# A decode step of a hybrid decoder in other parts: which engine forms the key-value product, who adds the old state, and when the decay is applied

## The chip, the cores and the metric

The kernel runs on one core of a Trainium2 chip. A core has five engines that run side by side and wait for each other by semaphores: TensorE (PE, matmuls and the weight loads that go with them), VectorE (DVE), ScalarE (ACT), GpSimd (POOL) and SyncE (SP). Transfers are issued from SP, ACT or POOL and carried out by 16 DMA engines. SBUF is the working memory of 128 partitions; TensorE writes to PSUM, which has eight banks. The metric is the device time of one execution in microseconds (us), as the median of the runs.

## The reference

Two layers of a trunk are applied to two groups that share all weights: a prompt of 512 tokens and eight sample tokens (one new token for each of eight sequences, with a state each).

```python
def retention_chunk(S, q, k, v, log_gamma):
    ...
    inter = jnp.einsum('blhd,bhde->blhe', q, S) * q_dec[None, :, :, None]
    k_dec = jnp.exp(log_gamma[None, :] * (L - 1.0 - idx[:, None]))
    S_new = (jnp.exp(log_gamma * L)[None, :, None, None] * S
             + jnp.einsum('blhd,blhe->bhde', k * k_dec[None, :, :, None], v))
    return S_new, intra + inter

def trunk_layer(x, p_i, pos, conv_buf, ret_S, norm_g, w_in, conv_w, gn_g, w_out, w_pg, w_ple):
    h = rmsnorm(x, norm_g)
    z = h @ w_in
    b_c, c_c, x_c, g_c, q, k, v, g_r = split_projection(z)
    conv_y, new_buf = short_conv(c_c * x_c, conv_buf, conv_w)
    y_conv = b_c * conv_y * jax.nn.silu(g_c)
    ...
    o, new_S = retention(q, k, v, ret_S.astype(jnp.float32), retention_log_gamma())
    ...
    x = x + jnp.concatenate([y_conv, y_ret], axis=-1) @ w_out
    x = x + jax.nn.sigmoid(x @ w_pg) * (p_i @ w_ple)
```

For a sample token (a chunk of length 1) this comes to one step for each of 4 heads h and 8 sequences b: the new state is S' = gamma_h S + k v, a 256 x 256 matrix, and the token's output of the retention is q S'. There are 32 such steps in a layer, 64 in all. gamma_h is 1 - 2^(-5-h). The new states are outputs of the kernel.

## The kernel before

Activations stand transposed in SBUF, 128 features by 520 tokens (512 of the prompt, 8 samples), one such tile to a *slot*. There are NSLOT = 75 slots of 520 columns; get() takes the one that has been free longest, put() gives it back. All matmuls of the layers are done in single precision by three passes: each operand is split into a high part (ScalarE copies it to the matmul's format, L229 for weights, L551 for activations) and a low part (VectorE subtracts, L230, L552). mm3 (L245 on) then makes three matmuls, L247 to L249, of a 128 x 128 weight tile with 260 columns. Most products of a pair of output tiles go by Strassen's scheme (strassen, one level, seven products), for which VectorE adds weight quarters (L319) and operands, and ScalarE copies PSUM banks out (L307). Weights come from HBM by SP's queue into a ring of 32 raw tiles, and their split parts go into a second ring, split_ring, of SPLIT = 60 tiles of 128 columns. A part of the ring is free again when the matmuls that read it are done.

A layer runs in this order: four heads of the retention (retain: projections for q, k, v and the gate, pair by pair), eight convolution groups, the output projection w_out, and the gate with w_pg and w_ple. In the last layer the last two tiles of the gate are done in another layout at the end. The chunks of the prompt's retention are queued as small steps (later, s0 to s8) between the projections' products.

The decode of the samples is put between the projections too. After a head's v has been made, its eight (h, b) go on the list todo. Function sample() is called in the middle of pairs and at their ends. Each call finishes the (h, b) that the call before loaded (sample_step) and starts the load of another (sample_load):

- sample_load takes two slots. st gets the old state by a transfer from sret (L770), 128 partitions of 512 numbers: rows of v (two halves e) by 256 columns of k. kb gets q and k of this token, 512 numbers spread over all partitions (L771, from kq). Both are issued from POOL.
- sample_step multiplies st by gamma_h on ScalarE (L776, the scale read from a column of vec), adds k times v for each half on VectorE (L780; vs holds v/16 per partition), sends st to o_rets (L781, from POOL), then multiplies by q and sums along the row into osum for each half on VectorE (L784), and gives both slots back.

When the convolution's last group is reached, what is left of the list is drained, and sample_norm uses osum.

The order of instructions on each engine is set by a planner that simulates the program with costs of its own, within the data's dependences; keep() marks instructions that stay in the program's order, and a few blocks have a higher priority. Every engine works off its own queue in that order, POOL's and SP's transfers too: an instruction that waits holds up all behind it. Waits are put in where an instruction needs data, or a slot or ring part that an earlier user has not yet released. Only at the end of the kernel is the order written by hand.

vec holds constants in 160 columns: gains, convolution weights, decays; columns 128 to 131 are the four gammas (gam).

Of the kernel before, what the change touches and what calls it, by code (L numbers as in the profile page):

```python
# [7 lines left out]
F32 = mybir.dt.float32  # L8
F32R = mybir.dt.float32r
AF = mybir.ActivationFunctionType  # L10
ALU = mybir.AluOpType
MUL, ADD, SUB = ALU.mult, ALU.add, ALU.subtract

P = 128
# [3 lines left out]
SEQ = 512  # L18
NS = 8
T = SEQ + NS  # L20
# [4 lines left out]
H = 4  # L25
# [1 line left out]
PLE = 256  # L27
PAST = 4096
EPS = 1e-6
NSLOT = 75  # L30
CH = 4
CHS = 4
CHA = 4
# [16 lines left out]
EARLY = 6  # L50


HEADS = [[0, 0, 0, 8] + [14] * 12, [0] + [14] * 15]
CONVS = [[14] * 2 + [16] * 13 + [14]] * 2
OUT_ROWS = [[0, 8, 16, 16, 16, 16, 16, 0]] * 2
# [6 lines left out]
RAW = 32  # L62
WARM = 8
FIRST = 8
SPLIT = 60


def F(ap):
# [11 lines left out]
class Slots:  # L80
# [8 lines left out]
    def get(self, dtype=F32):  # L89
        i = self.free.pop(0)  # L90
        self.count += 1
        t = self.pool.tile([P, T], dtype, tag=f"s{i}", name=f"slot{i}_{self.count}")
        self.used[id(t)] = (t, i)
        return t
# [97 lines left out]
def trunk_kernel(  # L192
# [6 lines left out]
    V, S, G, PE, DMA = nc.vector, nc.scalar, nc.gpsimd, nc.tensor, nc.sync  # L199
    SIDE = nc.gpsimd  # L200

    const = ctx.enter_context(tc.tile_pool(name="const", bufs=1))
# [5 lines left out]

    slots = Slots(spool, NSLOT)
    get, getr, put = slots.get, slots.getr, slots.put  # L210
# [6 lines left out]
    keep = tc.keep_in_program_order  # L217
# [340 lines left out]
        return op  # L558


    vec = const.tile([P, 160], F32, name="vec")

    def norm_g(l, k):
        return vec[:, 16 * l + k : 16 * l + k + 1]
# [11 lines left out]
    def kd(h, m):  # L576
        c = 112 + 4 * h + m
        return vec[:, c : c + 1]

    def gam(h):  # L580
        return vec[:, 128 + h : 129 + h]

    ident = const.tile([P, P], F32, name="ident")
    ones = const.tile([P, P], F32, name="ones")
# [4 lines left out]
    vs = const.tile([P, H, 2, NS], F32, name="vs")  # L589
    osum = const.tile([P, 2, H, NS], F32, name="osum")  # L590
# [84 lines left out]
    for a, b in ((0, 1), (1, 4), (4, 8), (8, 12), (12, 16)):  # L675
        raws = []
        if b == 1:
            raw = raw_ring.get(4)
            DMA.dma_start(raw.rearrange("p (m n) -> p m n", n=P), wi[0, 0:4, :, :P].rearrange("m p n -> p m n"))
            S.dma_start(vec, vecs)  # L680
            x = get()
            for n in (LEFT, RIGHT):
                DMA.dma_start(x[:, n], xT[0, :, n])
            xs.append(x)
            w = split_w(raw)
            ws = [[t[:, P * m : P * m + P] for t in w] for m in range(4)]
        else:
            for i in range(4):
                raws.append(load(wi[0, i, :, P * a : P * b]))
                if i < b - a:  # L690
                    x = get()
                    DMA.dma_start(x, xT[a + i])
                    xs.append(x)
            ws = [split_w(raw) for raw in raws]
            raw_ring.put(*raws)
        for k in range(a, b):
            X.ops[k] = split(xs[k], norm_g(0, k), free_src=False, halves=k % 2 == 0 and k < max(X.rows))
            for m in range(4):
                for h, n in enumerate((LEFT, RIGHT)):
                    product(first[m][h], ws[m], k - a, at(X.ops, [k], n), k == 0, k == KT - 1)  # L700
        if b == 1:
            raw_ring.put(raw)
            split_ring.put(*w)
            DMA.dma_start(ident, ident_d)
        else:
            for w in ws:
                split_ring.put(*w)
# [8 lines left out]
    for l in range(DEPTH):  # L716
# [24 lines left out]
        root, rb, rc, rs = prepare()  # L741
# [24 lines left out]
            return g  # L766

        def sample_load(h, b):
            st, kb = get(), get()
            SIDE.dma_start(st[:, :512], sret[l, h, b])  # L770
            SIDE.dma_start(kb[:, :512], kq[l, h, b].rearrange("c d -> (c d)").partition_broadcast(P))  # L771
            return h, b, st, kb

        def sample_step(h, b, st, kb):

            keep(S.activation(st[:, :512], st[:, :512], AF.Identity, scale=gam(h)))  # L776
            k = kb[:, 256:512]
            for e in range(2):
                c = slice(256 * e, 256 * e + 256)
                keep(V.scalar_tensor_tensor(st[:, c], k, vs[:, h, e, b : b + 1], st[:, c], MUL, ADD))  # L780
            SIDE.dma_start(o_rets[l, h, b], st[:, :512])  # L781
            for e in range(2):
                c = slice(256 * e, 256 * e + 256)
                V.tensor_tensor_reduce(k, st[:, c], kb[:, :256], 1.0, 0.0, MUL, ADD, osum[:, e, h, b : b + 1])  # L784
            put(st, kb)

        loaded = []

        def sample():

            if loaded:
                sample_step(*loaded.pop(0))
            if todo:
                loaded.append(sample_load(*todo.pop(0)))

        todo = []
# [20 lines left out]
        def retain(h):  # L817

            mt = 8 * h
            qks = small.tile([P, 4, 32], F32, tag="qks", name="qks")  # L820
            G.memset(qks, 0.0)


            if l == 0 and h == 0:
                q = rope(*first[:2])
            else:
                q = rope(*head(mt))
            for d in range(2):
                S.activation(qks[:, d, :NS], q[d][:, SEQ:T], AF.Copy)
            aside_copy(h, 0, q)  # L830


            if l == 0 and h == 0:
                kf = rope(*first[2:])
            else:
                kf = rope(*head(mt + 2))
            for d in range(2):
                S.activation(qks[:, 2 + d, :NS], kf[d][:, SEQ:T], AF.Copy)
            aside_copy(h, 2, kf)
            qkt = small.tile([P, 4, 32], F32, tag="qkt", name="qkt")  # L840
            V.transpose(qkt.rearrange("p a b -> p (a b)"), qks.rearrange("p a b -> p (a b)"))
            for g in range(4):
                SIDE.dma_start(kq[l, h, :, :, 32 * g : 32 * g + 32], qkt[32 * g : 32 * g + NS])


            vf = []
            for e, z in enumerate(head(mt + 4)):
                t = z.slot if z.ps is None else copied(z.ps).slot
                V.scalar_tensor_tensor(vs[:, h, e, :], t[:, SEQ:T], 1.0 / 16, rb[:, SEQ:T], MUL, MUL)
                vf.append(t)  # L850
            aside_copy(h, 4, vf)
            todo.extend((h, b) for b in range(NS))


            gts = [silu(z) for z in head(mt + 6)]
            for e, gt in enumerate(gts):
                S.activation(gs[:, 2 * h + e], gt[:, SEQ:T], AF.Copy)
            aside_copy(h, 6, gts)
            later.extend(steps(h))
# [217 lines left out]
        for j in range(CJ):  # L1077
# [12 lines left out]
            t = get()  # L1090
# [8 lines left out]
            if j < CJ - 1:  # L1099
                middle.append(sample)  # L1100
            if j == CJ - 1:
                while loaded or todo:
                    sample()
                O.ready = 7
                sample_norm(nc, small, pr, osum, onesd, half_neg, gs, lambda k: gn_g(l, k))
# [45 lines left out]
        for k in range(2):  # L1151
            t = get()
# [22 lines left out]
        for m in range(0, KT - tail, 2):  # L1175
# [19 lines left out]
            for i, z in enumerate(zs):  # L1195
                x = xs[i]
                t = get() if z.slot is None else z.slot
# [17 lines left out]
        if tail:  # L1215
# [30 lines left out]
            for j, n in enumerate(blocks):  # L1246
                c = slice(PC * j, PC * j + PC)
# [34 lines left out]
            for i in range(tail):  # L1282
# [6 lines left out]
                with tc.high_priority():  # L1289
                    sg, t = update(x, pes[i][:, n0], ps)  # L1290
# [188 lines left out]
```

## Time and profile before

| what | value |
|---|---|
| median of three runs | 2167.58 us |
| the three runs | 2167.56, 2167.58, 2169.25 us |
| span of the profiled execution | 2167.3 us |
| DMA traffic | 387.31 MB, mean 179 GB/s |
| chain that ended last, PE's share | 42% |

The table of times gives the profiled execution as its span, from the first to the last instruction of the program. A profile page gives the busy time of each engine, its queues, and groups of instructions by line of the kernel. L230 is line 230; `slot<-ps_g` says that a slot was written from a PSUM bank; x128 is the number of instructions. The views that go with it cut the time into windows, list who waited for whom, and list instructions in order of time. A releaser behind an arrow is what ended an engine's idle time. Matmuls overlap in their pipeline: a single one is shown with some 0.28 us, though they follow each other much faster.

### The profile page before, as it was taken

To read this page: it belongs to the slowest core of one execution; us is meant where nothing else is said; L and a number is where in the kernel's file an instruction comes from. 1 tells how busy PE (TensorE), PEld (TensorE's weight loads), DVE (VectorE), ACT (ScalarE), POOL (GpSimd) and SP (SyncE) were. 2 spreads that over 40 slices of the span, in tenths; PEclk is the share of its full clock that TensorE was granted. 3 is DMA by queue.
4 is the path that set the end of the run, shared out by engine and by line. 5 is a ranking of instruction groups with operands and counts; after the bars stand their busy time and mean duration, and the time that the engine had idled before them with its cause. 6 is when DMAs were issued, how large, how long until landed. Compare 5 with 4: busy or idle time off the path is not lost. (4 is left out here: it accounts for less than half of the span.)

```text
span 2167.3 us, 48178 instructions
## 1 busy us (share of the span) xinstructions
PE 2147.8 (99%) x17861; PEld 2142.1 (99%) x17861; DVE 1896.1 (87%) x3849; ACT 1264.5 (58%) x2647; POOL 430.6 (20%) x746
## 2 busy tenths in 40 slices
PE   9999999999999999999999999999999999999998
PEld 9999999999999999999999999999999999999998
DVE  8889988998999987987997988989999998879884
ACT  8656655565555655655765655565645555456565
POOL 2313222211001211200212222231111022011011
PEclk9999999999999999999999999999999999999999
DMA  8555565545543745645645566664464355566455
GB/s 288 171 175 197 181 217 184 178 157 175 158 129 118 238 156 187 215 154 160 215 144 175 172 213 191 189 209 170 151 182 149 120 158 202 176 207 200 128 164 198
DMA packets 182861, 387.31 MB, mean 179 GB/s; under 512 B 25888, under 2 KB 56352, under 8 KB 182624
## 3 DMA queue, kind: packets, MB, share of 16 engines
q1 hardware_dynamic: 128704, 212.98, 31.6%
q0 software_dynamic: 53056, 169.84, 23.8%
q8 instruction: 140, 2.29, 0.4%
q10 hardware_dynamic: 864, 1.39, 0.2%
q14 instruction: 97, 0.79, 0.1%
HBM read 318.96 MB, written 65.15 MB: 177 GB/s over the span
## 5 line engine op out<-in xcount | busy, mean ns | idle before, releaser
L247 PE MATMUL ps_g<-slot,split 128*128 128x260 f32 x5465 | 1531.6, 284 | 7.2 <-ACT slot L307 2.9
L248 PE MATMUL ps_g<-slot,split 128*128 128x260 f32 x5465 | 1534.3, 282 | 0.3 <-DVE slot L555 0.3
L249 PE MATMUL ps_g<-slot,split 128*128 128x260 f32 x5461 | 1519.9, 283 | 0.5 <-DVE split L230 0.5
L229 ACT ACTIVATE split<-raw 128x512 fp32r<-128x512 f32 (+2 forms) x1347 | 777.3, 596 | 583.1 <-DVE raw L319 213.2
L247 PEld LDWEIGHTS ps_g<-slot,split 128*128 128x128 f32 x5465 | 1024.0, 188 | 10.1 <-ACT slot L307 3.7
L248 PEld LDWEIGHTS ps_g<-slot,split 128*128 128x128 f32 x5465 | 1028.5, 188 | 0.5 <-DVE slot L555 0.5
L249 PEld LDWEIGHTS ps_g<-slot,split 128*128 128x128 f32 x5461 | 1019.8, 188 | 1.0 <-DVE split L230 1.0
L230 DVE TENSOR_TENSOR split<-raw,split 128x512 fp32r<-128x512 f32 (+2 forms) x1346 | 849.2, 652 | 172.5 <-PE ps_g L248 85.4
L319 DVE TENSOR_TENSOR raw<-raw 128x512 f32<-128x512 f32 (+1 forms) x660 | 428.9, 660 | 32.5 <-DMA raw<-wi 23.7
L307 ACT ACTIVATE slot<-ps_g 128x260 f32<-128x260 f32 x336 | 127.4, 381 | 140.6 <-PE ps_g L249 122.7
L551 ACT ACTIVATE slot<-slot 128x520 fp32r<-128x520 f32 (+1 forms) x212 | 109.2, 562 | 46.6 <-DVE slot L414 11.1
L552 DVE TENSOR_TENSOR slot<-slot,slot 128x520 fp32r<-128x520 f32 (+1 forms) x212 | 124.4, 620 | 4.1 <-ACT slot L551 3.9
L781 POOL DMA_DIRECT2D o_rets<-slot x64 | 35.3, 552 | 351.6 <-DVE slot L780 131.7
L307 DVE TENSOR_TENSOR slot<-ps_g,slot 128x260 f32<-128x260 f32 x168 | 70.9, 424 | 6.0 <-PE ps_g L249 3.7
L869 POOL DMA_DIRECT2D slot<-hs x64 | 46.2, 724 | 118.7 <-DVE split L230 42.7
L814 POOL DMA_DIRECT2D hs<-slot x64 | 35.6, 556 | 139.3 <-DVE slot L755 61.3
L780 DVE SCALAR_TENSOR_TENSOR slot<-slot,vs,slot 128x256 f32<-128x256 f32 x128 | 56.1, 481 | 4.5 <-ACT slot L776 4.3
L746 DVE TENSOR_TENSOR slot<-slot,slot 128x520 f32<-128x520 f32 x80 | 55.8, 698 | 4.7 <-DMA o_rets<-slot 3.7
L770 POOL DMA_DIRECT2D slot<-sret x64 | 35.5, 554 | 114.6 <-ACT split L229 37.3
L1058 POOL DMA_DIRECT2D slot<-x1s x76 | 40.8, 538 | 87.6 <-PE ps_g L249 27.2
L1209 POOL DMA_DIRECT2D x2s<-slot x30 | 16.4, 545 | 201.6 <-DVE slot L1204 200.6
L771 POOL DMA_DIRECT2D slot<-kq x64 | 34.9, 547 | 106.0 <-DVE slot L876 22.2
(217 smaller groups left out, 1733.8 us busy)
## 6 DMA issues: line engine op xcount, KB each, us to landing
raw<-wi SPq DMA_DIRECT2D x377, 256.0 KB, 3.9
raw<-wo SPq DMA_DIRECT2D x128, 256.0 KB, 5.4
raw<-wg SPq DMA_DIRECT2D x122, 256.0 KB, 4.1
raw<-wi SPq DMA_DIRECT2D x136, 192.0 KB, 4.0
slot<-x1s POOLq DMA_DIRECT2D x76, 260.0 KB, 5.1
slot<-sret POOLq DMA_DIRECT2D x64, 256.0 KB, 4.0
hs<-slot POOLq DMA_DIRECT2D x64, 256.0 KB, 4.0
slot<-hs POOLq DMA_DIRECT2D x64, 256.0 KB, 5.2
```

Of the source, the lines that this page charges most:

```text
L229: S.activation(hi, raw, AF.Copy)
L230: V.tensor_tensor(lo, raw, F(hi), SUB)
L247: PE.matmul(out, wh, xh, start=start, stop=False, skip_group_check=more)
L248: PE.matmul(out, wh, xl, start=False, stop=False, skip_group_check=more)
L249: PE.matmul(out, wl, xh, start=False, stop=stop, skip_group_check=more)
L307: fn(*args)
L319: V.tensor_tensor(out[:, n], x[:, n], y[:, n], op)
L551: keep(S.activation(hi, src[:, n], AF.Copy))
L552: V.tensor_tensor(lo, src[:, n], F(hi), SUB)
L746: V.tensor_tensor(out[:, n], v, table[:, n], MUL)
L780: keep(V.scalar_tensor_tensor(st[:, c], k, vs[:, h, e, b : b + 1], st[:, c], MUL, ADD))
L869: SIDE.dma_start(t[:, :512].rearrange("p (m n) -> p m n", m=2), src)
```

## The change

The step is put into three calls of sample() instead of two. sample_load brings only q and k. A new sample_add, one call later, takes a slot st, in which ScalarE writes k times v for each half (Copy with the scale per partition from vs), and POOL issues a transfer that adds the old state to it in SBUF (accum_op=ADD). sample_step, another call later, makes VectorE's two products with q and their sums, now with the factor gamma_h, then multiplies st by gamma_h on ScalarE and sends it to o_rets. For that vs holds v/16/gamma_h, so that gamma (S + k v/gamma) = gamma S + k v. The gammas are constants of the instructions, and vec is cut to 128 columns. NSLOT grows from 75 to 76, SPLIT falls from 60 to 56. The drain before sample_norm also empties the new list.

```diff
--- before.py
+++ after.py
@@ -27,7 +27,7 @@
 PLE = 256
 PAST = 4096
 EPS = 1e-6
-NSLOT = 75
+NSLOT = 76
 CH = 4
 CHS = 4
 CHA = 4
@@ -50,6 +50,7 @@
 EARLY = 6
 
 
+GAMMA = [1.0 - 2.0 ** (-5 - h) for h in range(H)]
 HEADS = [[0, 0, 0, 8] + [14] * 12, [0] + [14] * 15]
 CONVS = [[14] * 2 + [16] * 13 + [14]] * 2
 OUT_ROWS = [[0, 8, 16, 16, 16, 16, 16, 0]] * 2
@@ -62,7 +63,7 @@
 RAW = 32
 WARM = 8
 FIRST = 8
-SPLIT = 60
+SPLIT = 56
 
 
 def F(ap):
@@ -558,7 +559,7 @@
         return op
 
 
-    vec = const.tile([P, 160], F32, name="vec")
+    vec = const.tile([P, P], F32, name="vec")
 
     def norm_g(l, k):
         return vec[:, 16 * l + k : 16 * l + k + 1]
@@ -576,9 +577,6 @@
     def kd(h, m):
         c = 112 + 4 * h + m
         return vec[:, c : c + 1]
-
-    def gam(h):
-        return vec[:, 128 + h : 129 + h]
 
     ident = const.tile([P, P], F32, name="ident")
     ones = const.tile([P, P], F32, name="ones")
@@ -677,7 +675,7 @@
         if b == 1:
             raw = raw_ring.get(4)
             DMA.dma_start(raw.rearrange("p (m n) -> p m n", n=P), wi[0, 0:4, :, :P].rearrange("m p n -> p m n"))
-            S.dma_start(vec, vecs)
+            S.dma_start(vec, vecs[:, :P])
             x = get()
             for n in (LEFT, RIGHT):
                 DMA.dma_start(x[:, n], xT[0, :, n])
@@ -766,30 +764,36 @@
             return g
 
         def sample_load(h, b):
-            st, kb = get(), get()
-            SIDE.dma_start(st[:, :512], sret[l, h, b])
+            kb = get()
             SIDE.dma_start(kb[:, :512], kq[l, h, b].rearrange("c d -> (c d)").partition_broadcast(P))
-            return h, b, st, kb
-
-        def sample_step(h, b, st, kb):
-
-            keep(S.activation(st[:, :512], st[:, :512], AF.Identity, scale=gam(h)))
-            k = kb[:, 256:512]
+            return h, b, kb
+
+        def sample_add(h, b, kb):
+
+            st = get()
             for e in range(2):
                 c = slice(256 * e, 256 * e + 256)
-                keep(V.scalar_tensor_tensor(st[:, c], k, vs[:, h, e, b : b + 1], st[:, c], MUL, ADD))
-            SIDE.dma_start(o_rets[l, h, b], st[:, :512])
+                keep(S.activation(st[:, c], kb[:, 256:512], AF.Copy, scale=vs[:, h, e, b : b + 1]))
+            SIDE.dma_start(st[:, :512], sret[l, h, b], accum_op=ADD)
+            return h, b, kb, st
+
+        def sample_step(h, b, kb, st):
+
             for e in range(2):
                 c = slice(256 * e, 256 * e + 256)
-                V.tensor_tensor_reduce(k, st[:, c], kb[:, :256], 1.0, 0.0, MUL, ADD, osum[:, e, h, b : b + 1])
+                V.tensor_tensor_reduce(kb[:, 256:512], st[:, c], kb[:, :256], GAMMA[h], 0.0, MUL, ADD, osum[:, e, h, b : b + 1])
+            keep(S.activation(st[:, :512], st[:, :512], AF.Copy, scale=GAMMA[h]))
+            SIDE.dma_start(o_rets[l, h, b], st[:, :512])
             put(st, kb)
 
-        loaded = []
+        loaded, added = [], []
 
         def sample():
 
+            if added:
+                sample_step(*added.pop(0))
             if loaded:
-                sample_step(*loaded.pop(0))
+                added.append(sample_add(*loaded.pop(0)))
             if todo:
                 loaded.append(sample_load(*todo.pop(0)))
 
@@ -846,7 +850,7 @@
             vf = []
             for e, z in enumerate(head(mt + 4)):
                 t = z.slot if z.ps is None else copied(z.ps).slot
-                V.scalar_tensor_tensor(vs[:, h, e, :], t[:, SEQ:T], 1.0 / 16, rb[:, SEQ:T], MUL, MUL)
+                V.scalar_tensor_tensor(vs[:, h, e, :], t[:, SEQ:T], 1.0 / 16 / GAMMA[h], rb[:, SEQ:T], MUL, MUL)
                 vf.append(t)
             aside_copy(h, 4, vf)
             todo.extend((h, b) for b in range(NS))
@@ -1099,7 +1103,7 @@
             if j < CJ - 1:
                 middle.append(sample)
             if j == CJ - 1:
-                while loaded or todo:
+                while added or loaded or todo:
                     sample()
                 O.ready = 7
                 sample_norm(nc, small, pr, osum, onesd, half_neg, gs, lambda k: gn_g(l, k))
```

## The prediction

> **What bounds the kernel now.** I read the page first: how long the span is and which engine fills it.
>
> ```profile
> span 2167.3 us, 48178 instructions
> PE 2147.8 (99%) x17861; PEld 2142.1 (99%) x17861; DVE 1896.1 (87%) x3849; ACT 1264.5 (58%) x2647; POOL 430.6 (20%) x746
> ```
>
> PE is busy for 99% of the span. But matmuls are pipelined, so "busy" doesn't say that PE runs at its pace. The view by windows does: it gives the matmuls of each stretch of time. I cut it at the stages: heads and convolution of layer 0 (to 706), its output projection (to 920), its gate (to 1118), heads and convolution of layer 1 (to 1780), its output projection (to 1960) and gate (to 2134).
>
> ```profile
> 0.00:50.00 50.00, 47.24 (x364) 46.32 (x365) 40.33 (x77) 41.61 (x78) 14.51 (x35) 1.00 0.84 288
> 50.00:400.00 350.00, 350.00 (x2922) 349.45 (x2921) 313.66 (x687) 209.05 (x461) 95.92 (x166) 1.00 0.59 189
> 400.00:706.00 306.00, 304.31 (x2540) 303.93 (x2538) 279.85 (x561) 169.48 (x345) 44.48 (x67) 1.00 0.49 150
> 706.00:920.00 214.00, 211.42 (x1758) 211.00 (x1759) 186.95 (x357) 121.42 (x257) 42.35 (x79) 1.00 0.61 199
> 920.00:1118.00 198.00, 198.00 (x1651) 197.52 (x1650) 170.00 (x333) 127.58 (x250) 31.48 (x54) 1.00 0.53 168
> 1118.00:1500.00 382.00, 380.93 (x3182) 380.22 (x3181) 337.91 (x743) 222.73 (x495) 98.60 (x169) 1.00 0.60 187
> 1500.00:1780.00 280.00, 279.57 (x2331) 278.74 (x2330) 258.90 (x513) 157.30 (x325) 38.36 (x58) 1.00 0.49 149
> 1780.00:1960.00 180.00, 178.15 (x1482) 177.71 (x1482) 151.20 (x277) 98.54 (x202) 35.99 (x68) 1.00 0.61 205
> 1960.00:2134.00 174.00, 173.83 (x1447) 173.42 (x1445) 142.06 (x272) 103.17 (x207) 25.04 (x48) 1.00 0.51 165
> 2134.00:2168.00 34.00, 24.34 (x201) 23.80 (x200) 15.25 (x38) 13.65 (x36) 3.91 (x6) 0.94 0.49 173
> ```
>
> After the bounds come the stretch's length, then busy time and count of PE, its weight loads, DVE, ACT, POOL, then the granted clock. The gate of layer 0 is never idle: 1651 matmuls in 198.00 us, 0.1199 us each at clock 1.00. I take that as PE's pace. All 17861 matmuls at it take 2142.0 us, so only 2167.3 - 2142.0 = 25.3 us of the span are anything else. Stage by stage, length minus count times pace: 6.4 us in the first 50, 9.2 in the last 33.3 (to the span's end), 1.8 in the four stretches of heads and convolutions (-0.4, 1.4, 0.4, 0.5), 5.9 in the four of output and gate (3.2, 0.0, 2.3, 0.5). (That makes 23.3; matmuls across a bound are counted twice, 17 x 0.12 = 2.0.) **The change touches no matmul. Between 50 and 2134 us it can win back at most 1.8 + 5.9 = 7.7 us, and of that 1.8 where its steps run.** What it can lose has no such bound.
>
> The view of waits, for PE alone, and two rows of its timeline name these few stops (waited for, us in total, times, longest):
>
> ```profile
> PE ps_g L247 <- ACT slot L307: 2.9, 4, 1.3
> PE ps_g L247 <- ACT ps_g L307: 1.6, 2, 1.2
> PE ps_g L247 <- ACT split L229: 1.5, 2, 1.3
> ...
> PE ps_vt L913 <- DMA slot<-hs: 0.9, 1, 0.9
> ...
> 491.60 0.30 PE L913 MATMUL ps_vt<-ident,slot 128*128 128x128 f32 x1 [0.94 <-DMA slot<-hs]
> 1471.65 0.39 PE L248 MATMUL ps_st<-slot,slot 128*128 128x256 f32 x1 [0.46 <-DVE slot L918]
> ```
>
> PE waits mostly for ACT, which copies banks out (L307) and makes the high parts (L229); once, at 1471.65, for DVE in a sample stage.
>
> **The change, part by part.** Rows of the grouped lines and of single lines; after the bar, busy time and mean ns of one, then idle time before.
>
> ```profile
> L776 ACT ACTIVATE slot<-slot,vec x64: 706/713/722, 81.2 to 1713.3; 128x512 f32<-128x512 f32 x64
> L780 DVE SCALAR_TENSOR_TENSOR slot<-slot,vs,slot 128x256 f32<-128x256 f32 x128 | 56.1, 481 | 4.5 <-ACT slot L776 4.3
> L784 DVE CUSTOM_DVE_ANT_0 slot<-slot,slot 128x256 f32<-128x256 f32 x128 | 53.9, 421 | 0.0
> L229 ACT ACTIVATE split<-raw 128x512 fp32r<-128x512 f32 x1032 | 632.3, 626 | 462.3 <-DVE raw L319 188.2 <-PE ps_g L249 166.4 <-PE ps_g L248 45.1
> L229 ACT ACTIVATE split<-raw 128x256 fp32r<-128x256 f32 x66 | 27.3, 415 | 36.7 <-DMA raw<-wi 29.0 <-PE ps_g L248 5.2 <-PE ps_g L249 1.9
> L917 ACT ACTIVATE slot<-ps_kt,vec 128x256 fp32r<-128x256 f32 x32 | 15.0, 468 | 9.2 <-DMA hs<-slot 3.2 <-DVE slot L918 2.5 <-PE ps_kt L913 2.2
> ```
>
> *VectorE* loses 128 multiply-adds (L780) and their 56.1 us; the reducing products (L784) stay. In 400 to 706 it falls from 279.85 of 306.00 busy (91%) by about 0.44 per instruction. That work lay beside PE, so it is worth only the stops that hang on it: 0 to -1.8 us, the whole of the sample stages. A VectorE op ends just one stop there, the 0.46 at 1471.65: I take **-0.5**.
>
> *ScalarE* gets 128 products of 256 columns with a scale per partition. From SBUF with such a scale there is no row at that size. Without the scale L229 takes 0.415; the scale costs 0.713 - 0.626 = 0.09 at 512 columns (L776 against L229), so an estimate from these rows is 0.50; L917, out of PSUM with the scale, takes 0.468. The decay's scale becomes a constant, 64 x 0.09 = 5.6 us less. Net 128 x 0.50 - 5.6 = +58 us on an engine at 209.05 of 350.00 (60%) in 50 to 400. Its idle time hides that, unless the two products stand just ahead of a copy that PE awaits: then 1.0 us a time. With the four stops of the first wait row, 0 to +4; these lie mostly where the samples are done, so I take **0**.
>
> On this the Trainium skill speaks against the change: "ScalarE: Activation LUTs", section Rules for kernel authors, gives multiplication to VectorE. Here the two rows at 256 columns are close, and the rule ignores which engine is full. By it the sum would lose the -0.5 and gain nothing else.
>
> *The adding transfer.* No row shows one. The plain load and store that it is made of:
>
> ```profile
> DMA to landing us min/median/max: 2.8/4.0/7.3
> o_rets<-slot POOLq DMA_DIRECT2D x64, 256.0 KB, 3.1
> 1394.28 0.71 ACT L776 ACTIVATE slot<-slot,vec 128x512 f32<-128x512 f32 x1
> ...
> 1401.67 0.71 ACT L776 ACTIVATE slot<-slot,vec 128x512 f32<-128x512 f32 x1
> ```
>
> The first row is the load's (L770). If adding costs nothing it lands in 4.0 us; if it must read the slot as the store does, 4.0 + 3.1 = 7.1; above that no row bounds it. I take 7.1. It is issued one call of sample() ahead of its use. 64 steps lie between 81.2 and 1713.3; the two rows are one of the closest pairs, 7.4 us apart; so 7.1 is hidden nearly everywhere: **0**. If it took 15 us, VectorE's next product would wait at the head of its queue at the close pairs.
>
> "DMA: Bandwidth & Descriptors" of the Trainium skill, section Rules for kernel authors, says that an accumulate reads its destination and writes it later; no run here shows it. It would bear out the 7.1 rather than the 4.0 and leaves the sum.
>
> *The order and the waits.* Now ScalarE waits for a free slot before its products, POOL for ScalarE before the adding transfer, ScalarE for both reductions before the decay, POOL for the decay before the store. Before, the load alone waited for the slot, on POOL:
>
> ```profile
> L770 POOL DMA_DIRECT2D slot<-sret x64 | 35.5, 554 | 114.6 <-ACT split L229 37.3 <-PE ps_s L249 13.8 <-ACT slot L307 9.7
> L781 POOL DMA_DIRECT2D o_rets<-slot x64 | 35.3, 552 | 351.6 <-DVE slot L780 131.7 <-issue 81.3 <-ACT split L229 72.7
> ```
>
> POOL sat idle 114.6 us ahead of these loads and 351.6 ahead of the stores. On POOL that delays only fetches, of which one cost PE time (0.94 at 491.60). On ScalarE the splits (L229) and copies (L307) stand behind the wait. The slot is asked for one call later and ScalarE reaches it later, so I count nothing: **0**; its bounds are 0 and, where one step in five stops PE as in the two rows above (13 x 0.5 to 0.9), +12. The store leaves later by two reductions and the decay, 2 x 0.42 + 0.63 = 1.5 us, and its slot comes free as much later. The issues stay 192 on POOL, none on SP.
>
> *The ring of splits* falls from 60 to 56 tiles. A high and a low part of four tiles each feed 12 matmuls, 1.44 us of PE, so the full ring is 60/8 x 1.44 = 10.8 us ahead before and 10.1 after: 0.72 less, in every stage.
>
> ```profile
> ACT split L229 <- PE ps_g L249: 186.2, 220, 3.9
> ...
> DVE split L230 <- PE ps_g L248: 85.4, 109, 2.2
> ```
>
> These two waits are the full ring (the splitting engines wait for PE to free tiles): it is full often, so the reserve is real. It costs at most 0.72 at each stop that began with a full ring: 0 to 9 x 0.72 = +6.5 with the nine waits in the four PE rows above. I take the two that end on a split: **+1.4**. A sample step gives VectorE 2 x 0.44 = 0.88 back, about the same.
>
> *The slot more* is held by the pipeline (three slots per sample in flight instead of two); it is free in the output and gate stages, worth 0 to -5.9 there; no stop there names a slot, so **0**. The smaller vec is one load of 80 KB that becomes 64: nothing.
>
> Sum: 2167.3 - 0.5 + 1.4 = 2168.2 for the span. The median of the runs is 2167.58, 0.3 above the profiled span, so **2168.5**.
>
> **The rivals.** *Nothing to measure* (forecast): a change of less than 0.2%, 4.3 us, about what a measurement of this kernel can tell from none: 2163 to 2172. For it: PE at its pace in all stages, the terms small and of both signs. **0.62.**
>
> *Slower, by the new waits on ScalarE.* The wait for slot and reductions moves from POOL, where it cost nothing, to the queue on which most of PE's stops already end. It decides once ScalarE stands there longer than the ring's 10.1 us of reserve, or when the ring wasn't full. Price: 6 to 12 us with the ring's +1.4 to +6.5: 2175 to 2186. For it: the 114.6 us above, and an order on every queue that is laid anew, in a kernel with only 7.7 us of stops. Against it: ScalarE is idle 40%. **0.26.**
>
> *Faster.* VectorE's relief and the free slot clear the 1.8 and half to all of the 5.9: -4.8 to -7.7, so 2160 to 2163. Against it: the output stages' stops wait for ScalarE, which isn't relieved. **0.08.** The section Identifying the Most-Contended Engine of "Perfetto Trace Analysis" in the Trainium skill would give no gain either, since the fullest engine isn't relieved; the windows agree.
>
> *The transfer doesn't do what it should:* it lands after 15 us or more, VectorE stands at the close pairs for up to 15 - 7.4 = 7.6 us, which eats most of the ring's reserve; ten such pairs at 1 to 4 us past it give +10 to +40: 2178 to 2208. **0.04.**
>
> **How the numbers follow.** Faster 0.08, same 0.62, slower 0.26 + 0.04 = 0.30. The range reaches from 2162 (part of the faster case) to 2181 (more than half of the slower one), leaving some 0.05 below and 0.13 above.
>
> **What would show it.** Pace: 0.120 us per matmul again with some 17861 of them. VectorE's total lower by about 56, ScalarE's higher by about 58. The adding transfer's landing: 4 to 7 us. PE's waits: the stop on L918 gone, those on L229 and L307 no more than 2 us longer in sum. The forecast is wrong if PE's waits on ScalarE or on DMA grow by over 4 us between 81 and 1731, or if the stops at 706 to 730 and 1788 to 1796 vanish.

## The result, and the profile after

The changed kernel takes 2240.6 us (median of four runs, 2236.7 to 2244.0), beside 2168.4 for the kernel before on the same chip: **72.2 us slower**, ratio 1.0332 (95% interval 1.0318 to 1.0347). The prediction was 2168.5 with a range of 2162 to 2181. (Of the experiments below, 9 and 10 had one execution each that took far longer, 4246 and 11018 us; their figures leave it out.)

The head of the page, the new lines among the costliest groups, and the landing of the new transfer. In the changed kernel lines up to the sample steps stand one further down (splits L230 and L231, copies L308, weight sums L320, mm3's matmuls L248 to L250). L776 is the products, L777 the adding transfer, L784 the reductions, L785 the decay, L786 the store.

```profile
span 2240.5 us, 48468 instructions
PE 2171.7 (97%) x17861; PEld 2156.3 (96%) x17861; DVE 1849.3 (83%) x3721; ACT 1299.5 (58%) x2775; POOL 458.8 (20%) x746
...
L784 DVE CUSTOM_DVE_ANT_0 slot<-slot,slot 128x256 f32<-128x256 f32 x128 | 53.8, 420 | 123.1 <-DMA slot<-sret 122.8
L786 POOL DMA_DIRECT2D o_rets<-slot x64 | 35.6, 557 | 356.6 <-ACT slot L785 314.3
L777 POOL DMA_DIRECT2D slot<-sret x64 | 57.2, 894 | 47.9 <-ACT slot L308 18.1
L776 ACT ACTIVATE slot<-slot,vs 128x256 f32<-128x256 f32 x128 | 57.7, 499 | 9.7 <-issue 5.6
...
slot<-sret POOLq DMA_DIRECT2D x64, 256.0 KB, 6.3
```

The line to look at is the reductions'. Their work is what it was (0.42 us each), but VectorE sat idle for 123.1 us ahead of them, where it sat 0.0 before, and nearly all of it ended with the landing of the transfer from sret. The transfer lands in 6.3 us, less than the 7.1 that I took.

Where in time the loss lies, by windows at the same stages, each as long as its work now takes: heads and convolution of layer 0 (to 734), its output (to 948) and gate (to 1146), the same of layer 1 (to 1854, 2034, 2208).

```profile
50.00:734.00 684.00, 662.10 (x5462) 656.48 (x5461) 570.28 (x1188) 395.77 (x871) 154.64 (x231) 1.00 0.55 164
734.00:948.00 214.00, 212.70 (x1775) 212.49 (x1774) 186.86 (x354) 121.52 (x256) 42.96 (x80) 1.00 0.61 200
948.00:1146.00 198.00, 197.61 (x1642) 196.92 (x1642) 169.06 (x333) 127.81 (x251) 31.31 (x56) 1.00 0.54 169
1146.00:1854.00 708.00, 675.77 (x5512) 669.42 (x5512) 576.34 (x1197) 398.53 (x884) 150.76 (x226) 0.98 0.55 160
1854.00:2034.00 180.00, 177.73 (x1476) 176.94 (x1476) 151.37 (x273) 98.40 (x199) 34.41 (x65) 1.00 0.62 205
2034.00:2208.00 174.00, 172.96 (x1434) 172.18 (x1432) 140.09 (x269) 103.53 (x210) 24.77 (x47) 1.00 0.51 162
```

The output and gate stages are as long as before (214, 198, 180, 174). Heads and convolution of layer 0 went from 350 + 306 = 656 to 684, those of layer 1 from 382 + 280 = 662 to 708: +28 and +46, together 74. The whole loss lies in the two stages in which sample steps run. At the old pace of 0.1199 us the 5462 and 5512 matmuls fill 654.9 and 660.9 us of them. Most of the loss is PE standing: it is idle for 21.9 and 32.2 us there, where it was idle for 1.7 and 1.5 before. But its busy time exceeds the old pace too, by 7.2 and 14.9 us, and about half of that is a lower clock (the figure of 0.98 in the fourth row). Three windows around the longest stop, just before it, in it and after it:

```profile
1376.00:1385.00 9.00, 9.00 (x77) 9.00 (x77) 2.84 (x6) 3.42 (x9) 1.44 (x3) 1.00 0.72 218
1386.00:1391.00 5.00, 0.10 (x2) 0.10 (x1) 1.77 (x7) 1.03 (x4) 0.08 (x1) 0.78 0.72 188
1391.00:1395.00 4.00, 4.00 (x19) 4.00 (x20) 4.00 (x8) 1.91 (x4) 2.74 (x4) 0.50 0.52 142
```

PE stood for 4.9 us; then the granted clock was 0.50, and some 4.8 matmuls came per us instead of 8.6. Six such stretches, 27.3 us in all, lie in these two stages, each at or just after a stop of PE; the kernel before has none there. At half the pace they cost some 12 us of the 74 (an estimate from their length). Not every stop brings one: after the 1.59 us at 619.56, shown below, the clock stayed at 1.00.

The waits, first of PE, then of the engines behind it:

```profile
PE ps_g L248 <- DVE slot L308: 16.9, 16, 1.7
PE ps_g L248 <- ACT slot L308: 13.3, 9, 4.9
PE ps_g L248 <- ACT ps_g L308: 13.1, 14, 3.0
PE ps_s L249 <- DVE slot L880: 7.5, 4, 3.2
...
ACT split L230 <- DVE raw L320: 263.8, 152, 10.2
DVE split L231 <- ACT split L230: 143.9, 178, 5.8
DVE slot L784 <- DMA slot<-sret: 122.8, 50, 6.5
...
ACT slot L785 <- DVE osum L784: 10.4, 4, 3.3
```

PE's four largest waits come to 50.8 us, where the four rows shown of before came to 6.9. They end on copies, not on the sample steps; one has to go back along the queues. One stop, in the timeline (start, duration, engine, line, and idle time before it in brackets):

```profile
607.77 0.87 POOL L777 DMA_DIRECT2D slot<-sret  x1 [0.26 <-ACT slot L776]
...
610.96 0.68 DVE L231 TENSOR_TENSOR split<-raw,split 128x512 fp32r<-128x512 f32 x1
615.13 0.43 DVE L784 CUSTOM_DVE_ANT_0 slot<-slot,slot 128x256 f32<-128x256 f32 x1 [3.48 <-DMA slot<-sret]
...
617.15 1.42 DVE L320 TENSOR_TENSOR raw<-raw 128x512 f32<-128x512 f32 x2
618.49 0.68 DVE L231 TENSOR_TENSOR split<-raw,split 128x512 fp32r<-128x512 f32 x1
619.09 0.42 DVE L308 TENSOR_TENSOR slot<-ps_g,slot 128x260 f32<-128x260 f32 x1
...
618.68 0.63 ACT L230 ACTIVATE split<-raw 128x512 fp32r<-128x512 f32 x1 [4.68 <-DVE raw L320]
...
619.56 0.39 PE L248 MATMUL ps_g<-slot,split 128*128 128x260 f32 x1 [1.59 <-DVE slot L308]
```

POOL issues the adding transfer at 607.77. VectorE is through with its splits at 611.6, and the next thing in its queue is the reduction of this same state. It stands until the state has landed, 7.4 us after the issue. Behind the reduction in VectorE's queue are the weight sums (617.15), for which ScalarE's high part waits 4.68 us, and an add of a bank (619.09), for which PE waits 1.59. So a wait for a transfer, on an engine that is 83% busy, comes out at PE under other names.

This pair is no exception. Over all 64 steps VectorE came to the first reduction a median of 4.2 us after the issue (the reduction's start less the idle time ahead of it), and 58 times sooner than the 6.3 us of the landing. In the kernel before, a median of 31.9 us lay between the issue of the load and the first reduction.

### The profile page after: what moved, and what is told of

The parts are those of the page before. It is cut to its first block, busy times and chain, and to the rows that moved or that the text cites. A ratio compares the mean times of both kernels' runs of the same rounds, so it can differ in the third digit from the quotient of the medians.

```text
span 2240.5 us, 48468 instructions
## 1 busy us (share of the span) xinstructions
PE 2171.7 (97%) x17861; PEld 2156.3 (96%) x17861; DVE 1849.3 (83%) x3721; ACT 1299.5 (58%) x2775; POOL 458.8 (20%) x746
## 5 line engine op out<-in xcount | busy, mean ns | idle before, releaser
L248 PE MATMUL ps_g<-slot,split 128*128 128x260 f32 x5461 | 1539.5, 285 | 47.0 <-DVE slot L308 16.9
L250 PE MATMUL ps_g<-slot,split 128*128 128x260 f32 x5461 | 1534.2, 283 | 0.8 <-DVE split L231 0.8
L230 ACT ACTIVATE split<-raw 128x512 fp32r<-128x512 f32 (+2 forms) x1346 | 777.6, 596 | 689.3 <-PE ps_g L249 266.4
L248 PEld LDWEIGHTS ps_g<-slot,split 128*128 128x128 f32 x5461 | 1027.6, 189 | 57.4 <-DVE slot L308 20.5
L250 PEld LDWEIGHTS ps_g<-slot,split 128*128 128x128 f32 x5461 | 1029.1, 189 | 1.5 <-DVE split L231 1.3
L231 DVE TENSOR_TENSOR split<-raw,split 128x512 fp32r<-128x512 f32 (+2 forms) x1346 | 845.1, 646 | 169.7 <-ACT split L230 143.9
L320 DVE TENSOR_TENSOR raw<-raw 128x512 f32<-128x512 f32 (+1 forms) x660 | 422.5, 655 | 30.2 <-DMA raw<-wi 26.7
L784 DVE CUSTOM_DVE_ANT_0 slot<-slot,slot 128x256 f32<-128x256 f32 x128 | 53.8, 420 | 123.1 <-DMA slot<-sret 122.8
L308 ACT ACTIVATE slot<-ps_g 128x260 f32<-128x260 f32 x336 | 124.3, 372 | 44.0 <-PE ps_g L250 31.1
L786 POOL DMA_DIRECT2D o_rets<-slot x64 | 35.6, 557 | 356.6 <-ACT slot L785 314.3
L308 DVE TENSOR_TENSOR slot<-ps_g,slot 128x260 f32<-128x260 f32 x168 | 70.8, 422 | 3.4 <-PE ps_g L250 2.1
L777 POOL DMA_DIRECT2D slot<-sret x64 | 57.2, 894 | 47.9 <-ACT slot L308 18.1
L776 ACT ACTIVATE slot<-slot,vs 128x256 f32<-128x256 f32 x128 | 57.7, 499 | 9.7 <-issue 5.6
```

Source lines behind the costliest of these rows:

```text
L230: S.activation(hi, raw, AF.Copy)
L231: V.tensor_tensor(lo, raw, F(hi), SUB)
L248: PE.matmul(out, wh, xh, start=start, stop=False, skip_group_check=more)
L250: PE.matmul(out, wl, xh, start=False, stop=stop, skip_group_check=more)
L308: fn(*args)
L320: V.tensor_tensor(out[:, n], x[:, n], y[:, n], op)
```

## The experiments

Differences are medians against the kernel before, measured beside each on the same chip (2167.4 for experiments 1 to 4; 2168.2, 2169.5 and 2169.6 for the others). The theory after reading the trace: VectorE stands at the reductions because they come too soon after the transfer. The rivals: the smaller ring; ScalarE's products and decay, which stand ahead of its splits and copies; a loss from new order and memory alone; the transfer's own work.

**1. No adding.** The transfer writes the state over the product.

```diff
-            SIDE.dma_start(st[:, :512], sret[l, h, b], accum_op=ADD)
+            SIDE.dma_start(st[:, :512], sret[l, h, b])
```

> The changed kernel with a plain load in place of the adding transfer: the old state overwrites the product, so the new states and the samples' sums lack k times v. Every engine's order of instructions is the changed kernel's. Theory A (VectorE's reductions stand in its queue for the landing of the adding transfer, 6.3 us; 122.8 us of waiting in 50 waits): a plain load lands in about 4 us, the wait falls by some 50 x 2.3 us to 10 to 40 us, and the time to 2175 to 2205 us. Rival B (the ring of 56 tiles) and rival C (ScalarE's products and decay ahead of its splits and copies): nothing of theirs is changed, the time stays at 2233 to 2245 us.

Measured 2191.7, +24.3 (ratio 1.011, 1.0095 to 1.0125). The order on every engine is that of the changed kernel. The wait and the landing of this kernel:

```profile
DVE slot L784 <- DMA slot<-sret: 62.6, 38, 4.3
...
DMA to landing us min/median/max: 2.7/4.7/7.8
```

The changed kernel's landing row, for comparison:

```profile
DMA to landing us min/median/max: 3.9/6.3/8.7
```

With the same order and a landing 1.6 us shorter, two thirds of the loss go (72.2 - 24.3 = 47.9). ScalarE's products and decay are all still there, so they are not these two thirds. Half of the wait is left (62.6 of 122.8, more than the 10 to 40 expected), yet only a third of the loss. Two things fit that: the ring's reserve takes up short stops and not long ones (not shown), and of the six stretches at clock 0.50 only one, of 3.4 us, is left.

**2. The reductions held in the program's order.** Before, the multiply-adds that used the loaded state carried keep(), the reductions behind them did not. The change removed the multiply-adds, and with them the only thing on VectorE that held the use of the state in its place. (ScalarE's decay was kept as well; before, it stood ahead of the multiply-adds, now it comes behind the reductions.)

```diff
-                V.tensor_tensor_reduce(kb[:, 256:512], st[:, c], kb[:, :256], GAMMA[h], 0.0, MUL, ADD, osum[:, e, h, b : b + 1])
+                keep(V.tensor_tensor_reduce(kb[:, 256:512], st[:, c], kb[:, :256], GAMMA[h], 0.0, MUL, ADD, osum[:, e, h, b : b + 1]))
```

> The changed kernel with the reductions held in program order on VectorE, behind everything that the program has given VectorE before them, so that the planner can't move them up to the moment at which it takes the adding transfer as landed. Theory A: VectorE's waits for the state's transfer fall from 122.8 us to under 20, and the time to 2163 to 2180 us. Rivals B and C: the ring, the products and the decay stay, so it stays above 2220 us.

Measured 2191.1, +23.7 (1.0111, 1.0096 to 1.0126). The same step, the 29th of 64, in this kernel's timeline, and the kernel's waits:

```profile
605.25 0.87 POOL L777 DMA_DIRECT2D slot<-sret  x1 [0.26 <-ACT slot L776]
...
622.16 0.41 DVE L784 CUSTOM_DVE_ANT_0 slot<-slot,slot 128x256 f32<-128x256 f32 x1
```

```profile
PE ps_g L248 <- ACT ps_g L308: 8.2, 7, 3.6
PE ps_g L248 <- ACT slot L308: 6.6, 6, 2.0
...
ACT slot L785 <- DVE osum L784: 47.0, 31, 3.1
...
DVE slot L784 <- DMA slot<-sret: 28.0, 14, 3.3
```

Now 16.9 us lie between issue and reduction (median of the 64 steps 15.7, and 12 of them under 6.3), and VectorE waits 28.0 us instead of 122.8. With the adding left in, 72.2 - 23.7 = 48.5 us are back. The expectation of 2163 to 2180 was too good: 24 us stay. This and experiment 1 are two ways to shorten the same wait, one by the landing and one by the order, and each gives 48 us. **The stand at the reductions is shown to cost two thirds of the loss.** The two 48 us are the same ones and do not add; experiment 15 has both.

**3 and 4. The memory alone,** in the kernel before: the ring of 56 by itself, and then all that the change does to memory and constants (NSLOT 76, vec of 128 columns, gammas as constants) with the old step.

```diff
-SPLIT = 60
+SPLIT = 56
```

> The kernel before with a ring of splits of 56 tiles instead of 60, and nothing else. Theory A: 2165 to 2174 us (my prediction had +1.4, bounds 0 to +6.5). Rival B: most of the 72 us shows here, 2200 us or more.

```diff
-NSLOT = 75
+NSLOT = 76
...
-SPLIT = 60
+SPLIT = 56
...
-    vec = const.tile([P, 160], F32, name="vec")
+    vec = const.tile([P, P], F32, name="vec")
...
-        return vec[:, 128 + h : 129 + h]
+        return 1.0 - 2.0 ** (-5 - h)
...
-            S.dma_start(vec, vecs)
+            S.dma_start(vec, vecs[:, :P])
```

> The kernel before with all that the change does to memory: ring of 56, 76 slots, vec of 128 columns, the gammas as constants; the step itself as before. Theory A: 2163 to 2174 us. Rival B: 2200 us or more.

Measured +27.4 (1.0128, 1.0109 to 1.0146) and +34.1 (1.0156, 1.0139 to 1.0173). Waits of the kernel before with the ring of 56:

```profile
ACT split L229 <- PE ps_g L248: 331.7, 371, 3.9
DVE split L230 <- ACT split L229: 186.9, 220, 4.8
...
PE ps_g L247 <- ACT split L229: 11.2, 13, 2.1
```

PE waits for ScalarE's splits 11.2 us instead of 1.5. So the old step with four tiles less is 27 us slower, far more than 0.72 us at a few stops, and far less than the 72. That ScalarE finds the ring full 371 times, for 331.7 us, does not by itself say why: the same row has 416 times and 324.1 us with a ring of 64 (experiment 10), which is no slower than the kernel before. At equal memory the changed step with held reductions came out 10.4 us ahead, 2191.1 against 2201.5, a difference that another order alone can make (experiments 8 and 9).

**5 and 6. The ring back to 60,** in the changed kernel and in the one with held reductions.

```diff
-SPLIT = 56
+SPLIT = 60
```

> The changed kernel with the ring of splits back at 60 tiles; step, slots and vec as changed. The runs so far give two causes that add: the memory (before with the change's memory: +34 us) and the reductions that wait for the adding transfer (the rest, +39). If they add, this gives 2203 to 2215 us, and VectorE still waits some 120 us for the adding transfer. If the ring is beside the point and any new plan of the order costs some 25 to 35 us, it stays at 2230 to 2245 us.

> The changed kernel with both causes taken away: reductions held in program order, ring of 60. If ring and reductions are the two causes: 2158 to 2172 us. If any new plan of the order costs some 25 us: 2185 to 2200 us, as with the ring of 56.

Measured +74.0 (1.0349, 1.0332 to 1.0367) and +27.0 (1.012, 1.0105 to 1.0136). Both missed the range for two causes that add and fell into the other one, in which any new order costs some 25 to 35 us. The ring, worth 27 us in the old step, is worth nothing in the new one; costs found one at a time do not add up here. But the pair repeats experiment 2 with the other ring. The wait of the changed kernel with the ring of 60, and then with held reductions as well:

```profile
DVE slot L784 <- DMA slot<-sret: 123.5, 53, 5.3
```

```profile
PE ps_g L248 <- ACT slot L308: 12.0, 11, 2.9
PE ps_g L248 <- ACT ps_g L308: 4.1, 4, 1.9
...
DMA to landing us min/median/max: 3.9/4.8/7.8
```

Holding the reductions saves 74.0 - 27.0 = 47.0 us again.

**7 to 10: what another order costs by itself.** If the ring's cost is its size, 57 should stand near 56, and 61 and 64 no worse than 60; if it is how long ago a part was freed, 57 should stand near 60. The constants alone (gammas as numbers of the instruction) change no resource at all, only what the planner lays out.

```diff
-SPLIT = 60
+SPLIT = 57
```

> The kernel before with a ring of 57 tiles. Worked out from the ring's rule (it gives the part that has been free longest, chunks of 3 and 4 tiles by turns), a part was freed at least 13 releases earlier with 57 and with 60 tiles, and 11 with 56. If it is this distance: 2166 to 2178 us. If it is the size alone: 2186 to 2196 us, near that of 56.

```diff
-        return vec[:, 128 + h : 129 + h]
+        return 1.0 - 2.0 ** (-5 - h)
...
-            keep(S.activation(st[:, :512], st[:, :512], AF.Identity, scale=gam(h)))
+            keep(S.activation(st[:, :512], st[:, :512], AF.Copy, scale=gam(h)))
```

> The kernel before with the gammas as constants of the instruction (64 times some 0.09 us less on ScalarE) and all else as before, which makes the planner lay a new order. If ring and reductions are the causes: 2163 to 2172 us. If any new plan of the order costs some 25 us: 2185 to 2200 us.

```diff
-SPLIT = 60
+SPLIT = 61
```

> The kernel before with a ring of 61 tiles, more than it had. If what the smaller rings cost (56: +27 us, 57: +21) was the missing reserve, this is no slower than before: 2160 to 2170 us. If it was the new order that the planner lays for any other allocation, this is slower too: 2173 to 2200 us.

and the same edit with 64:

> The kernel before with a ring of 64 tiles. Missing reserve: 2158 to 2170 us. New order: 2173 to 2200 us.

| kernel before with | ratio | 95% interval |
|---|---|---|
| SPLIT 56 | 1.0128 | 1.0109 to 1.0146 |
| SPLIT 57 | 1.0096 | 1.0081 to 1.0111 |
| gammas as constants (SPLIT 60) | 1.0034 | 1.0021 to 1.0047 |
| SPLIT 61 | 1.0042 | 1.0025 to 1.0059 |
| SPLIT 64 | 0.9985 | 0.9976 to 0.9995 |

The constants cost 7.3 us, between their two ranges: the new order costs something, but not 25 us every time. One tile of ring more costs 0.42%, four more bring 0.15%. No lack of reserve explains that 61 is worse than 60, or that constants cost time. What all five share is that the planner lays out every queue anew, and with PE busy 99% of the time four of the five came out worse. But the size is not ruled out below 60: 57 stands near 56, as it should if the size counts, and while 61 fell into the range for a new order, 64 fell into that for missing reserve. What the times follow is how long PE waits for split parts, high and low together: 12.7, 9.3, 2.0, 6.1 and 1.1 us with rings of 56, 57, 60, 61 and 64. Whether size or order makes PE wait so is not separated; this is a reading of five runs, not a mechanism followed from wait to wait. The ring of 64 is the only version that came out ahead of the kernel before, by less than one can rely on.

**11 to 14. What is left with held reductions** (some 24 us): the decay one call later, the decay without keep(), the slot of the sent state given back one call later, or the adding transfer put ahead of the step before it. Three of them take one slot more.

```diff
...
+        def sample_out(h, b, st):
             keep(S.activation(st[:, :512], st[:, :512], AF.Copy, scale=GAMMA[h]))
             SIDE.dma_start(o_rets[l, h, b], st[:, :512])
-            put(st, kb)
+            put(st)
...
+            if reduced:
+                sample_out(*reduced.pop(0))
...
-                sample_step(*added.pop(0))
+                reduced.append(sample_step(*added.pop(0)))
```

> The changed kernel with reductions in program order and ring of 56 as in the run with held reductions (2191 us), and the decay and the store moved to one more call of sample(), with one slot more (77) for the state that waits. ScalarE's decay then meets reductions that were done a call ago. If the 47 us that ScalarE stood before the decay are what keeps that kernel 24 us above the one before: 2168 to 2178 us, and this wait under 5 us. If they are not, and the rest is what a new order of the plan costs: 2186 to 2200 us, with the wait gone all the same.

```diff
-            keep(S.activation(st[:, :512], st[:, :512], AF.Copy, scale=GAMMA[h]))
+            S.activation(st[:, :512], st[:, :512], AF.Copy, scale=GAMMA[h])
```

> The changed kernel with held reductions and ring of 56 (2191 us), but the decay is no longer pinned behind everything that ScalarE got before it, so the planner may place it. If ScalarE's stand before the decay is the rest: 2170 to 2182 us with less of that wait. If not: 2184 to 2200 us.

```diff
-            put(st, kb)
+            put(kb)
+            sent.append(st)
...
+            if sent:
+                put(sent.pop(0))
```

> The changed kernel with held reductions (2191 us), but the state's slot is given back one call of sample() after its store was issued, with one slot more (77). There ScalarE stood 20 us for slots whose store had not yet read them. If that is part of the 24 us that this kernel lies above the one before: 2176 to 2186 us, and this wait under 8 us. If not: 2188 to 2198 us with the wait gone.

```diff
-            if added:
-                sample_step(*added.pop(0))
+            n = len(added)
             if loaded:
                 added.append(sample_add(*loaded.pop(0)))
+            if n:
+                sample_step(*added.pop(0))
```

> The changed kernel with held reductions (2191 us), but each call of sample() first makes the product and the adding transfer of one sample and then finishes the other, with one slot more (77), so that the adding transfer doesn't stand behind the other's store on POOL. There VectorE still stood 28 us, in 14 waits, for adding transfers. If late adding transfers are part of the 24 us: 2174 to 2186 us, and the wait under 10 us. If not: 2188 to 2198 us.

Measured +23.6 (1.0106, 1.0089 to 1.0123), +25.4 (1.0119, 1.0104 to 1.0134), +25.8 (1.0124, 1.0108 to 1.014) and +24.4 (1.0116, 1.0099 to 1.0133): no difference from experiment 2. In the first, ScalarE's 47.0 us of waiting for reductions is gone and the time is the same, so that wait is not what is left. The second decides nothing by itself, since that wait rose to 57.9. Neither the decay's place nor the slot's return nor the transfer's place in the call gave anything back, as far as one can tell beside what another order may cost.

**15. The adding alone, with held reductions:** experiments 1 and 2 together, with the order of experiment 2 on every engine.

```diff
-            SIDE.dma_start(st[:, :512], sret[l, h, b], accum_op=ADD)
+            SIDE.dma_start(st[:, :512], sret[l, h, b])
```

> The changed kernel with held reductions and a plain load in place of the adding transfer, in the same order on every engine; the new states and the samples' sums lack k times v. If adding costs time of its own, beyond the reductions that stood in its way, this is faster than 2191 us by 5 us or more. If adding is as good as free once nothing stands for it: 2187 to 2194 us.

Measured 2182.2, +12.6 (1.0062, 1.0038 to 1.0086). The landing in this kernel:

```profile
DMA to landing us min/median/max: 2.7/3.4/7.6
```

and in experiment 2's:

```profile
DMA to landing us min/median/max: 3.9/4.4/8.6
```

Adding costs 23.7 - 12.6 = 11 us even where the order gives it more time (the two intervals leave 5 to 17). Part of that is still the stand: VectorE waits 28.0 us for the adding transfer here and 14.3 for the plain one. The four kernels together:

| | adding | plain |
|---|---|---|
| reductions free | +72.2 | +24.3 |
| reductions held | +23.7 | +12.6 |

Adding alone costs 11.1 us, free reductions alone 11.7, and both together 59.6: so 36.8 us come only when a later landing meets an earlier use. The 12.6 that are left stay open. They are near what another order cost the kernel before (+7.3 with the constants), but no run isolates it. A part of what is left in experiment 2 is the clock again: in its profiled execution it was 0.50 for 17.1 us, some 8 us of work, and in that of experiment 15, the fastest of its four, not at all before the last 33 us.

## Why the prediction was wrong

- **Pace and bounds: right, but for the clock.** PE again needs 0.12 us per matmul outside the stretches at clock 0.50, the output and gate stages kept their length, and what could be won back was nothing. The prediction had the clock at 1.00 throughout and no term for a lower one after stops (some 12 us). That the loss "has no such bound" was the half of that sentence that counted.
- **VectorE's relief: right in size, without worth.** The multiply-adds are gone (VectorE's total 1896.1 to 1849.3, 46.8 less; where the rest of the 56.1 went was not followed). An engine that is 83% busy stopped PE more often than when it was 87% busy, because of where it stood.
- **ScalarE's products: right.** 0.499 us each for the 0.50 estimated from the nearest rows; 128 x 0.499 - 64 x (0.714 - 0.622) = +58 by durations. The page's total rose by 35, since it counts time in which two instructions overlap once. Nothing shows that it cost PE time.
- **The adding transfer: the step that failed.** The landing was right (7.1 taken, 6.3 measured). Wrong was "It is issued one call of sample() ahead of its use" and so "7.1 is hidden nearly everywhere: **0**". In the program as written a call lies between them, 7.4 us at one of the closest pairs. But only kept instructions are held to that order. The multiply-adds were kept, the reductions never were. The prediction took the removal of the multiply-adds as 56.1 us of work less and did not ask what else they did: they held the use of the state in its place. Without them the planner moved the reductions up to the transfer: in the stop shown, VectorE got there 611.6 - 607.8 = 3.8 us after the issue, over all 64 steps a median of 4.2. The landing takes 6.3, and VectorE waited 50 times, 122.8 us in all. In place of 0 the term is +48.5 by experiment 2 (47.0 by 5 against 6, 47.9 by the other way of experiment 1); with all that the adding costs it is 59.6 (15).
- **The rivals.** The last one, at 0.04, named the right engine and the right wait, VectorE at the head of its queue, but made it depend on a landing of 15 us or more. With the use moved next to the issue, 6.3 did, and the loss still went 33 us beyond its range (2178 to 2208). The first slower rival looked to ScalarE's new waits: ScalarE waited 10.4 us for the reductions in the changed kernel, and the 47.0 of experiment 2 cost nothing when the decay came a call later (experiment 11). Ahead of its products ScalarE sat idle 9.7 us in all. It was not that. The direction was this rival's, with 2175 to 2186, but not its mechanism.
- **The ring: mis-sized.** "+1.4", with a bound of +6.5; alone in the kernel before it was +27.4. The sum assumed that the order stays and only the reserve shrinks. The order does not stay, and how the 27.4 divide between the two is open. In the changed kernel the same four tiles were worth nothing (5 and 6).
- **The slot and vec: not shown alone.** With ring and constants they came to +34.1 on the old step, 6.7 above the ring alone, about the constants' own 7.3.
- **The signs named beforehand.** "PE's waits on ScalarE or on DMA grow by over 4 us" was the one that showed: the two rows on L308 alone went from 4.5 to 26.4.

The Trainium skill's rule that the prediction kept out of its sum, "DMA: Bandwidth & Descriptors", section Rules for kernel authors (an accumulate reads its destination and writes it later), fits the landings, 1.6 us longer in one order and 1.0 in the other; the runs do not show how the time divides into reading and writing.

## What to carry to other kernels

Where a planner sets the order, "issued a call earlier" is no distance in time: look for what pins the use of a transfer, and when an instruction that carried the pin is removed, pin what now uses the data. Read the wait at the consumer's line (0.0 us before, 123.1 after) before any total of an engine's work. In this kernel, whose bounding engine is 99% busy, edits that take nothing away (constants, one tile of ring more) cost 0.3 and 0.4% by the new order alone; so set such a neutral edit beside the change, before a cause is sought in the edit's own arithmetic. And look at the granted clock where the bounding engine stands: here some stops cost more than their length.

## What the runs showed of the hardware

- An adding transfer from POOL takes 0.894 us to issue, where the plain load from sret took 0.554, and lands 1.0 us (4.4 against 3.4) or 1.6 us (6.3 against 4.7) later in the same order of instructions.
- How soon a transfer lands depends on the order around it as much as on the adding: the plain one landed in 3.4 us with held reductions and in 4.7 without, the adding one in 4.4 and 6.3. With the ring of 60 the adding one landed in 4.8 with held reductions and in 5.7 without. I had expected one landing time for each kind.
- Waits do not count in proportion: with the order unchanged, 62.6 us of them (38 waits, at most 4.3) went with a loss of 24.3 us and 122.8 us (50 waits, at most 6.5) with 72.2.
- Some stops of PE cost more than their length here: six times in the changed kernel's sample stages the granted clock was 0.50 for 3.4 or 6.8 us at a stop (4.8 matmuls per us instead of 8.6 in the one shown), in experiment 1 once, in the kernel before not at all.
